# Output blocks and layer 1's q, k transposed by DMA, and score matmuls that alternate between the array's halves

## The chip, the cores and the metric

The kernel runs on one core of a Trainium2 chip. The engines named below are TensorE (PE; PEld is its weight load), VectorE (DVE), ScalarE (ACT), GpSimd (POOL) and SyncE (SP), which here issues nearly all DMAs. The metric is the device time of one execution in microseconds. The time before is 2124.01 us, the median of 3 runs (2122.88 to 2124.37).

## The reference

A decoder trunk of two layers over 256 positions of 2048 features, batch 1, in float32. Layer 0 mixes by sliding-window attention (16 heads of 64, four to a key head) beside an mLSTM; layer 1 by a causal attention with forget gates (16 heads of 128). Each layer then has a SwiGLU feed-forward part with 5632 hidden features. Cut to what matters here:

```python
def sliding_window_attention(q, k, v, sinks):          # HEAD_DIM = 64, window 128
    scores = jnp.einsum('bnqhgd,bnkhd->bnhgqk', qb, kb) * (HEAD_DIM ** -0.5)
    scores = scores - slopes * dist.astype(jnp.float32)
    ...
def forgetting_attention_mixer(xn, w_in, b_f, w_out):  # FOX_HEAD_DIM = 128
    proj = xn @ w_in
    q, k, v, f = split_cols(proj, FOX_SIZES)
    ...
        s = jnp.einsum('bhqd,bhkd->bhqk', qb, k) * scale
        s = s + cb[..., None] - c[:, :, None, :]
    ...
    return out @ w_out
def swiglu(xn, w_gate, w_up, w_down):
    return (jax.nn.silu(xn @ w_gate) * (xn @ w_up)) @ w_down

for layer in range(2):
    xn = rms_norm(h, norm_mix[layer])
    mix = swa_mlstm_mixer(xn, ...) if layer == 0 else forgetting_attention_mixer(xn, ...)
    h = h + mix
    h = h + swiglu(rms_norm(h, norm_ffn[layer]), w_gate[layer], w_up[layer], w_down[layer])
return rms_norm(h, norm_final)
```

## The kernel before

**Precision and tiles.** Every large product is made of float32 values split into a high and a low part (type fp32r): three matmuls, high by high, high by low and low by high, in place of one. The residual `h` lies in SBUF as 2 row tiles of 128 positions by 2048 features. Matmuls contract over features on the partitions, so their left operand has to lie with features on the partitions: `xh`, `xl` hold the scaled input in that form, 16 tiles of 128 features by 256 positions, and `mh`, `ml` the mixer's or the hidden layer's output.

**Weights.** `load_raw` (L103) issues a DMA from SP of a chunk, 256 rows by 512 columns; `split_chunk` (L158) makes `hi` on ACT (L161) and `lo` on DVE (L162). There are 4 raw buffers and 6 of each split form. `gemm` (L177) walks the chunks, 12 matmuls each (L192 to L194); `project` runs 8 chunks into 2 accumulators of 128 by 512.

**How work is ordered.** The engines have queues of their own. The order of instructions on each is fixed when the kernel is built, by a planner that plays the program through with its own model of times; an instruction of a later piece of code may so stand before one of an earlier piece. In addition, the code keeps lists of work that falls due later: an entry is a step number and a function, and `run_due` (L172) calls it when the loop reaches that step, placed after the latest cast of a weight chunk.

**From rows to columns.** There are two ways. One is on TensorE: eight matmuls against an identity make four tiles of a block of 512 features in PSUM (L245 in `split_scaled`, L306 in `transpose_many`), which ACT and DVE then scale, split or copy out. The other is by DMA: the float32 block is taken apart on ACT into two planes of 16-bit halves (L272, or L521 in the feed-forward part), four transposing DMAs on SP turn them (L274, L523), and later a `join` on ACT puts the halves together again (L279, L528) and hands the block on. `split_turned` (L268) is this second way for a block of `h`; `scrap` (L284) gives it its two buffers, borrowed from the pool of the feed-forward part.

**Output projection.** `out_proj` (L386) runs two passes over pairs of blocks of 512 features, (0, 1) and (2, 3). In a pass both blocks do 6 chunks each, then the last 2 chunks each. After a block, `add_out` adds it into `h`. Blocks 0 and 1 go by `split_turned`, with their joins due at steps 6 and 10 of the second pass (`LATER`); blocks 2 and 3 go by `split_scaled` on TensorE.

**Feed-forward part.** `ffn` (L473) has three parts of 3, 4 and 4 groups of 512 hidden features, each followed by two groups of the down projection. A group (`pair_group`, L409) takes 8 pairs of feature tiles in the order `ORDER`. A plain pair is 24 matmuls. A mixed pair, marked 1 in `ORDER`, works with sums and differences of tiles and of weights (7 products instead of 8, so 21 matmuls): it needs sums of the pair's columns (`sums_of`, into `sx`) and four more subtractions and two more splits of the weights on DVE and ACT. Its products use the four PSUM banks that the plain accumulators of the group before had. After the last pair, the products are added into `c` (L466 to L470), the plain accumulators too (L494), and `silu` and the product are formed. A group's result is turned by DMA, with the join in the next group.

**Layer 1's attention.** For each of 4 groups of 4 heads (L910 to L938): project q, transpose it on TensorE into `qt`, project k, transpose it into `kt`, project v, then `attention` (L309).

**Scores.** `attention` works on 4 heads. It takes heads 0 and 2 first, then 1 and 3: for each such half, two narrow score matmuls (L316, 128 keys), one DVE instruction, two wide ones (L323, 256 keys), one DVE instruction. Each float32 matmul shows as two instructions. In layer 0 a head has 64 rows, and head j lies in rows 0 to 63 for even j and 64 to 127 for odd j of the partitions (`half_of`).

## Time and profile before

| What | us |
|---|---|
| Median of 3 runs | 2124.01 |
| Profiled execution, its own time | 2122.88 |
| Its span, first instruction to last | 2121.2 |
| PE, busy | 2105.2 |
| DVE, busy | 1719.5 |
| ACT, busy | 1277.0 |
| One transpose of a q or k block of layer 1 (L306, 64 in all), listed mean | 0.272 |
| One transpose of a block of `h` (L245, 88 in all), listed mean | 0.300 |
| Plane copy and joining copy of a block of the hidden layer, each of two | 1.04 and 1.35 |
| Transposing DMA, issue to landing, median (100 in all) | 2.5 |
| Weight chunk of 512 KB, issue to landing, median | 3.6 to 4.8 |

The span is the time from the first instruction to the last in one profiled execution; the execution took 1.7 us more. Busy times of engines overlap, so they don't add up. A listed length of an instruction is from its start to its end; on TensorE the next one starts before the last has ended, so the same line can be listed long and cost little. In a row of the list of groups, "x64" is the number of instructions. The granted TensorE clock is 0.999 of full speed throughout.

### The profile page before, as it was taken

The page shows a single profiled execution, that of the slowest core. Times are in us where ns is not written, and L with a number is a line of the kernel's source. Part 1 is how long each engine was busy: PE and PEld are TensorE (multiplying, and loading weights), DVE is VectorE, ACT ScalarE, POOL GpSimd, SP SyncE. Part 2 cuts the span into 40 slices and gives each one's busy share as a digit, 9 for nine tenths or more (in the row PEclk, how much of TensorE's full clock was granted, in tenths as well). Part 3 has the DMA queues.
Part 4 walks back from the last instruction along what each step waited for, and adds up shares of the span by engine and source line. Part 5 has one row for each costly group of instructions (what it writes and reads, how often), then busy time and mean ns, then how long its engine had stood idle before and what let it go on. Part 6 is the DMA issues. An engine that isn't in the chain of part 4 may idle for free.

```text
span 2121.2 us, 26858 instructions
## 1 busy us (share of the span) xinstructions
PE 2105.2 (99%) x9699; PEld 1747.9 (82%) x9699; DVE 1719.5 (81%) x2212; ACT 1277.0 (60%) x1612; POOL 39.6 (2%) x61
## 2 busy tenths in 40 slices
PE   8999999999999999999999999999999999999998
PEld 7888888888888888888888888888888888888886
DVE  6665558999999999999855554579999999989994
ACT  6565457765567656766645544576755667556763
POOL 2110000000000000000000000000000000000000
PEclk9999999999999999999999999999999999999999
DMA  8454547666567666666575564676656666656754
GB/s 267 145 157 149 170 149 268 209 203 215 191 211 225 215 207 216 209 202 215 163 231 168 169 179 140 194 237 210 215 196 208 218 196 224 225 188 212 224 182 147
DMA packets 267942, 421.48 MB, mean 199 GB/s; under 512 B 67136, under 2 KB 75424, under 8 KB 267552
## 3 DMA queue, kind: packets, MB, share of 16 engines
q1 hardware_dynamic: 267136, 416.02, 61.6%
q0 software_dynamic: 624, 3.72, 0.5%
q8 instruction: 76, 1.25, 0.2%
q14 instruction: 58, 0.48, 0.1%
q10 hardware_dynamic: 48, 0.02, 0.0%
HBM read 404.48 MB, written 2.11 MB: 192 GB/s over the span
## 4 chain that ended last, share of the span: by engine, by line
PE 98%; ACT 1%; issue 0%; DMA 0%; DVE 0%; DVEq 0%; POOLq 0%; POOL 0%; ACTq 0%
PE acc L402 17%; PE acc L403 17%; PE acc L404 17%; PE acc L192 10%; PE acc L193 10%; PE acc L194 10%; PE prod L402 4%; PE prod L403 4%; PE prod L404 4%; PE p L323 1%; PE ptm L306 1%; PE po L374 1%; PE pt L245 0%; PE pp L366 0%; PE p L316 0%
## 5 line engine op out<-in xcount | busy, mean ns | idle before, releaser
L161 ACT CAST hi<-raw 128x1024 fp32r<-128x1024 f32 (+2 forms) x681 | 692.5, 1032 | 598.5 <-PE acc L404 307.6
L162 DVE TENSOR_TENSOR lo<-raw,hi 128x1024 fp32r<-128x1024 f32 (+2 forms) x681 | 807.3, 1201 | 259.5 <-ACT hi L161 256.2
L403 PE MATMUL acc<-lo,xh 128*128 128x512 f32 x946 | 368.1, 389 | 0.0
L402 PE MATMUL acc<-hi,xh 128*128 128x512 f32 x946 | 367.4, 389 | 0.0
L404 PE MATMUL acc<-hi,xl 128*128 128x512 f32 x946 | 366.8, 389 | 0.0
L192 PE MATMUL acc<-hi,xh 128*128 128x512 f32 (+3 forms) x736 | 275.8, 377 | 0.8 <-ACT hi L161 0.8
L193 PE MATMUL acc<-lo,xh 128*128 128x512 f32 (+3 forms) x736 | 275.8, 375 | 0.0
L194 PE MATMUL acc<-hi,xl 128*128 128x512 f32 (+3 forms) x736 | 275.5, 376 | 0.0
L404 PEld LDWEIGHTS acc<-hi,xl 128*128 128x128 f32 x946 | 177.6, 188 | 36.9
L402 PEld LDWEIGHTS acc<-hi,xh 128*128 128x128 f32 x946 | 177.5, 188 | 36.8
L403 PEld LDWEIGHTS acc<-lo,xh 128*128 128x128 f32 x946 | 177.6, 188 | 36.7
L403 PE MATMUL acc<-lo,mh 128*128 128x512 f32 x437 | 170.0, 389 | 0.0
L402 PE MATMUL acc<-hi,mh 128*128 128x512 f32 x437 | 168.1, 389 | 0.0
L404 PE MATMUL acc<-hi,ml 128*128 128x512 f32 x437 | 167.9, 389 | 0.0
L192 PEld LDWEIGHTS acc<-hi,xh 128*128 128x128 f32 x736 | 138.7, 189 | 24.8 <-ACT hi L161 1.2
L193 PEld LDWEIGHTS acc<-lo,xh 128*128 128x128 f32 x736 | 139.0, 189 | 24.2 <-issue 0.9
L194 PEld LDWEIGHTS acc<-hi,xl 128*128 128x128 f32 x736 | 138.8, 189 | 24.5 <-issue 0.8
L295 DVE TENSOR_TENSOR lt<-raw,ht 128x1024 fp32r<-128x1024 f32 x95 | 115.9, 1220 | 15.6 <-ACT ht L294 15.6
L294 ACT CAST ht<-raw 128x1024 fp32r<-128x1024 f32 x95 | 99.8, 1050 | 45.7 <-PE acc L404 26.9
L192 PE MATMUL acc<-hi,mh 128*128 128x512 f32 x320 | 125.3, 392 | 1.2 <-ACT mh L294 1.2
L193 PE MATMUL acc<-lo,mh 128*128 128x512 f32 x320 | 125.3, 392 | 0.0
L194 PE MATMUL acc<-hi,ml 128*128 128x512 f32 x320 | 123.9, 390 | 0.0
(313 smaller groups left out, 3120.4 us busy)
## 6 DMA issues: line engine op xcount, KB each, us to landing
raw<-in_w_gate_dram SPq DMA_DIRECT2D x176, 512.0 KB, 4.4
raw<-in_w_up_dram SPq DMA_DIRECT2D x176, 512.0 KB, 4.7
raw<-in_w_down_dram SPq DMA_DIRECT2D x176, 512.0 KB, 4.8
raw<-in_w_in_odd_dram SPq DMA_DIRECT2D x88, 512.0 KB, 3.9
raw<-in_w_in_even_dram SPq DMA_DIRECT2D x64, 512.0 KB, 4.1
raw<-in_w_out_even_dram SPq DMA_DIRECT2D x32, 512.0 KB, 3.6
raw<-in_w_out_odd_dram SPq DMA_DIRECT2D x32, 512.0 KB, 4.1
raw<-in_w_in_odd_dram SPq DMA_DIRECT2D x8, 272.0 KB, 2.8
```

The source lines that it names most:

```text
L161: latest[0] = nc.scalar.copy(hi[:, :, 0:n], raw[:, :, 0:n])
L162: nc.vector.tensor_tensor(out=lo[:, :, 0:n], in0=raw[:, :, 0:n], in1=hi[:, :, 0:n].bitcast(F32), op=ALU.subtract)
L192: nc.tensor.matmul(o, ah[:, ts], hi, start=(k == 0), stop=False)
L193: nc.tensor.matmul(o, ah[:, ts], lo, start=False, stop=False)
L194: nc.tensor.matmul(o, al[:, ts], hi, start=False, stop=(k == k_all - 1))
L294: nc.scalar.copy(dst_h, src)
L295: nc.vector.tensor_tensor(out=dst_l, in0=src, in1=dst_h.bitcast(F32), op=ALU.subtract)
L306: nc.tensor.transpose(pt[:, i, :], s_, ident)
L323: nc.tensor.matmul(p1[:, jj, :], q_of(j, 1), k_of(j), start=True, stop=True)
L402: nc.tensor.matmul(o, ah, hi, start=start, stop=False)
L403: nc.tensor.matmul(o, ah, lo, start=False, stop=False)
L404: nc.tensor.matmul(o, al, hi, start=False, stop=stop)
```

## The change

Four things are changed.

1. In layer 1, q and k of the first three groups of heads are turned by DMA, by a new function `turn`, with the join due at step 6 of the projection that follows. The fourth group stays on TensorE.
2. In `out_proj`, blocks 2 and 3 go by `split_turned` too. Their joins are handed to the feed-forward part and fall due at positions 3 and 5 of its first group. `scrap` gives block 2 the buffer of block 0 and block 3 the two buffers of `sd`, which are allocated later and share their tag.
3. `ORDER` has its mixed pairs at positions 1, 3, 5 (pairs 1, 3, 5) in place of 2, 4, 6 (pairs 2, 3, 6).
4. `attention` first issues the narrow score matmuls of heads 0, 1, 2, 3, in two PSUM tiles by parity, and the two DVE instructions for them, then the wide ones likewise.

```diff
-ORDER = ((0, 0), (0, 1), (1, 2), (0, 4), (1, 3), (0, 5), (1, 6), (0, 7))
+ORDER = ((0, 0), (1, 1), (0, 2), (1, 3), (0, 4), (1, 5), (0, 6), (0, 7))
...
-LATER = (6, 10)
+AHEAD = 6
+LATER = (6, 10, 3, 5)
...
     def scrap(fp, n):
-        if n == 0:
+        if n % 2 == 0:
             box = fp.tile([P, 4, NB], F32, tag="c", name="box", bufs=1)
             halves = box[:, 0:2, :], box[:, 2:4, :]
+        elif n == 3:
+            halves = [fp.tile([P, 3, NB], F32, tag=f"sd{i}", name="box", bufs=1)[:, 0:CK, :] for i in range(2)]
         else:
...
         s = sp.tile([P, 4, 3 * P], F32, tag="s", name="s", bufs=2)
-        for half in range(2):
-            hs = slice(half, 4, 2)
-            p0 = pm.tile([P, 2, P], F32, tag="pm", name="p0")
-            for jj in range(2):
-                j = 2 * jj + half
-                nc.tensor.matmul(p0[:, jj, :], q_of(j, 0), k_of(j)[:, 0:P], start=True, stop=True)
-            nc.vector.scalar_tensor_tensor(
-                out=s[:, hs, 0:P], in0=p0, scalar=scale, in1=bias0[:, hs, :], op0=ALU.mult, op1=ALU.add
-            )
...
+        for b, cols, bias in ((0, P, bias0), (1, S, bias1)):
+            pq = [pm.tile([P, 2, cols], F32, tag="pm", name=f"p{b}") for _ in range(2)]
+            for j in range(4):
+                nc.tensor.matmul(pq[j % 2][:, j // 2, :], q_of(j, b), k_of(j)[:, 0:cols], start=True, stop=True)
+            for half in range(2):
+                hs = slice(half, 4, 2)
+                nc.vector.scalar_tensor_tensor(
+                    out=s[:, hs, b * P : b * P + cols],
+                    in0=pq[half],
...
     def out_proj(w, idx, key, extra):
-        last = KT - 4
+        last, rest = KT - 4, []
...
-                if n0 == 0:
-                    later.append((LATER[i], split_turned(idx, i, *scrap(extra[2], i), extra)))
-                else:
-                    split_scaled(idx, n0 + i, extra)
+                (later if n0 == 0 else rest).append(
+                    (LATER[n0 + i], split_turned(idx, n0 + i, *scrap(extra[2], n0 + i), extra))
+                )
                 square_sum(key, n0 + i)
+        return rest
...
-    def ffn(layer, fp, sx, sd, key, idx_next=None, key_next=None, finish=None):
+    def ffn(layer, fp, sx, sd, key, todo, idx_next=None, key_next=None, finish=None):
...
-            todo = []
             for g in range(g0, g1):
...
-            sd = [fp.tile([P, nd, 4, P], F32R, name=f"sd{i}", bufs=1) for i in range(2)]
-            out_proj(w_out, idx, key, (*sx, fp))
-            ffn(layer, fp, sx, sd, key, **rest)
+            todo = out_proj(w_out, idx, key, (*sx, fp))
+            sd = [fp.tile([P, nd, 4, P], F32R, tag=f"sd{i}", name=f"sd{i}", bufs=1) for i in range(2)]
+            ffn(layer, fp, sx, sd, key, todo, **rest)
...
+        def turn(src, dst):
+            planes = od.tile([P, 2, NT, NB], U16, tag="planes", name="planes")
+            turned = od.tile([P, 2, 4, NT, P], U16, tag="turned", name="turned")
+            su = src.bitcast(U16).rearrange("p t (n b) -> p t n b", b=2)
+            for b in range(2):
+                nc.scalar.copy(planes[:, b, :, :], su[:, :, :, b])
+                for t in range(NT):
+                    nc.sync.dma_start_transpose(turned[:, b, :, t, :], planes[:, b, t, :])
+
+            def join():
+                du = dst.rearrange("p k s -> p (k s)").bitcast(U16).rearrange("p (n b) -> p n b", b=2)
+                for b in range(2):
+                    nc.scalar.copy(du[:, :, b], turned[:, b, :, :, :].rearrange("p k t q -> p (k t q)"))
+
+            return join
+
         for i in range(4):
...
                 n_ = nat1(project(wi1, off + i * NB, NB), NB, "qk")
+                if i < 3:
+                    later.append((AHEAD, turn(n_, dst)))
+                    continue
```

More of the change, by code (lines that the diff above doesn't have):

```diff
@@ L310, in attention @@
         s = sp.tile([P, 4, 3 * P], F32, tag="s", name="s", bufs=2)
-        for half in range(2):
-            hs = slice(half, 4, 2)
-            p0 = pm.tile([P, 2, P], F32, tag="pm", name="p0")
-            for jj in range(2):
-                j = 2 * jj + half
-                nc.tensor.matmul(p0[:, jj, :], q_of(j, 0), k_of(j)[:, 0:P], start=True, stop=True)
-            nc.vector.scalar_tensor_tensor(
-                out=s[:, hs, 0:P], in0=p0, scalar=scale, in1=bias0[:, hs, :], op0=ALU.mult, op1=ALU.add
-            )
-            p1 = pm.tile([P, 2, S], F32, tag="pm", name="p1")
-            for jj in range(2):
-                j = 2 * jj + half
-                nc.tensor.matmul(p1[:, jj, :], q_of(j, 1), k_of(j), start=True, stop=True)
-            nc.vector.scalar_tensor_tensor(
-                out=s[:, hs, P : 3 * P], in0=p1, scalar=scale, in1=bias1[:, hs, :], op0=ALU.mult, op1=ALU.add
-            )
+        for b, cols, bias in ((0, P, bias0), (1, S, bias1)):
[7 more added lines that the diff above has]
+                    in0=pq[half],
+                    scalar=scale,
+                    in1=bias[:, hs, :],
+                    op0=ALU.mult,
+                    op1=ALU.add,
+                )
         parts = (slice(0, P), slice(P, 3 * P))
@@ L394, in out_proj @@
                 add_out(accs[i], n0 + i)
-                if n0 == 0:
-                    later.append((LATER[i], split_turned(idx, i, *scrap(extra[2], i), extra)))
-                else:
-                    split_scaled(idx, n0 + i, extra)
+                (later if n0 == 0 else rest).append(
+                    (LATER[n0 + i], split_turned(idx, n0 + i, *scrap(extra[2], n0 + i), extra))
+                )
                 square_sum(key, n0 + i)
+        return rest
     def three(o, ah, al, hi, lo, start, stop):
```

## The prediction

> **What bounds the kernel now.** I read the page's busy times and its chain first: which engine the end waits for.

> ```profile
> PE 2105.2 (99%) x9699; PEld 1747.9 (82%) x9699; DVE 1719.5 (81%) x2212; ACT 1277.0 (60%) x1612; POOL 39.6 (2%) x61
> PE 98%; ACT 1%; issue 0%; DMA 0%; DVE 0%; DVEq 0%; POOLq 0%; POOL 0%; ACTq 0%
> ```

> TensorE is busy for 2105.2 of 2121.2 us and is 98% of the chain, so a microsecond of its work that goes is a microsecond of time, as long as the others keep supplying it. A listed matmul time is not its cost, though: instructions overlap. The cost is the distance between starts, read in the timeline of PE around the transposes of one query block (start, length, instruction):

> ```profile
> 1076.02 0.39 PE L193 MATMUL acc<-lo,xh 128*128 128x512 f32 x1
> 1076.25 0.38 PE L306 MATMUL ptm<-ident,qk 128*128 128x128 f32 x2
> 1076.38 0.48 PE L194 MATMUL acc<-hi,xl 128*128 128x512 f32 x1
> 1076.70 0.39 PE L192 MATMUL acc<-hi,xh 128*128 128x512 f32 x1
> ...
> 1077.16 0.39 PE L194 MATMUL acc<-hi,xl 128*128 128x512 f32 x1
> 1077.39 0.82 PE L306 MATMUL ptm<-ident,qk 128*128 128x128 f32 x6
> 1077.96 0.48 PE L192 MATMUL acc<-hi,xh 128*128 128x512 f32 x1
> 1078.28 0.39 PE L193 MATMUL acc<-lo,xh 128*128 128x512 f32 x1
> ```

> Undisturbed, matmuls start 0.227 us apart. With two transposes between, L194 comes 0.36 after L193 and its successor 0.32 later: 0.13 + 0.09 lost. With six, L192 comes 0.80 after L194 and its successor 0.32 later: 0.57 + 0.09. Eight transposes cost 0.88 us; no wait for data is in it.

> Then the same for one sliding-window attention, whose heads have 64 rows:

> ```profile
> 69.23 0.39 PE L194 MATMUL acc<-hi,xl 128*128 128x512 f32 x1
> 69.55 0.71 PE L316 MATMUL p<-ks,qt 64*128 64x128 f32 x4
> 70.10 0.38 PE L323 MATMUL p<-ks,qt 64*128 64x256 f32 x1
> 70.10 0.37 PE L316 MATMUL p<-ks,qt 64*128 64x128 f32 x1
> ...
> 70.65 1.03 PE L323 MATMUL p<-ks,qt 64*128 64x256 f32 x5
> 71.61 0.50 PE L192 MATMUL acc<-hi,xh 128*128 128x512 f32 x1
> ```

> At 70.10 an L323 of heads 0, 2 and an L316 of heads 1, 3 start together: the two halves of the array work at once, but the second half starts only 0.55 us after the first.

> Last, what feeds PE: the waits (us in total, times, longest), the timelines of SP and ACT round one existing turn by DMA, and the stage table for one feed-forward group at the start and one in the middle.

> ```profile
> ACT hi L161 <- PE acc L404: 307.6, 211, 3.5
> SPq L523 <- ACT c L521: 62.0, 20, 4.2
> ```

> ```profile
> 437.07 5.45 SPq L523 DMA_TRANSPOSE turned<-c  x4
> 436.00 2.00 ACT L521 COPY c<-c 128x1024 uint16<-128x1024 uint16 x2 [0.48 <-DVE c L498]
> 451.02 2.56 ACT L528 COPY c<-turned 128x1024 uint16<-128x1024 uint16 x2
> ```

> ```profile
> 353.00:394.00 41.00, 41.00 (x185) 34.00 (x183) 39.15 (x56) 27.25 (x35) 0.69 (x1) 1.00 0.63 200
> 634.00:675.50 41.50, 41.50 (x185) 34.38 (x184) 39.82 (x51) 28.52 (x32) 0.00 (x0) 1.00 0.69 215
> ```

> Casts wait for PE to release one of six chunk buffers: ACT runs up to six chunks ahead, 6 x 12 matmuls x 0.227 = 16 us. Columns three to six of the table are PE, PEld, DVE, ACT: in the groups DVE is 96% busy (39.82 of 41.5), nearly a second bound, ACT only 69%.

> **Transposes.** They go for q and k of three groups of layer 1 (6 blocks) and for output blocks 2, 3 of both layers (4 blocks): 80 instructions. Six blocks at 0.88 are 5.3; the four output blocks, read in the same way, are 0.90, 0.90, 0.98 and 0.89, 3.7 together: **-9.0 us**. [...]

> What replaces them, per block: two plane copies on ACT (2.00), four transposing DMAs on SP (5.45), the last landing about 2.5 after its issue, two joining copies (2.56). ACT gains 4.56 x 10 = 46 us, DVE loses twelve L307 copies of 0.69 (8 us), the SP queue gets 40 issues (54 us). DVE's scaled splits at the layer ends stay (0.48 from either source). None is on the path while the lead holds:

> *SP.* Behind a transpose that waits for its planes stand weight loads. Held 4.2 (the longest wait so far) + 5.45 = 9.7 us, they use up the four raw buffers ahead (4 x 2.72 = 10.9, less 4 of landing) and then 2.8 of the 16 us of split chunks. Twenty existing turns do so with no gap on PE.

> *Layer 1.* A k block has nat1 2 x 0.69 + 2.00 + landing 6.7 (437.07 to 443.75) + 2.56 = 12.6 us before its attention, and the v projection takes 96 x 0.227 = 21.8: 9 us of slack; q has 31. ACT is 8.64 of 22 us busy here. The join stands in ACT's order behind the cast of chunk 6; if the DMA has not landed, later casts queue behind it for at most 6.7 us, within 16.

> *Layer ends.* Block 2 is ready 5.4 us before the last output matmul, block 3 with it. Two adds 1.36, planes 2.00, landing 6.7, join 2.56, scaling 4 x 0.5 make 14.6 us: ready at +9 and +15, SP's second four adding 5. First use is pair 4 (+20.4 us, 90 matmuls) and pair 6 (+30.6). ACT's load in that group rises from 27.25 by about 9 (one block's planes 2.0, two joins 5.1, half of the scaling) to 36 of 41 us. Waits for two landings (13.4) would make 50, 9 over; the lead covers that barely. Bounds per layer: 0 and 9 us; I take 0.3, since the existing joins of blocks 0, 1 load ACT likewise (41.95 of 57 us in 296 to 353) and PE shows no gap. **+0.6 in both.**

> **Score matmuls.** The four attentions cost, against undisturbed matmuls, 2.26, 2.75, 2.26, 2.99: 10.3 us (69.23 to 71.61 is 2.38, less 0.227, plus 0.11 on the next). The longer ones are split, their last four L323 issued later. One half's own work is 4 x 0.111 + 4 x 0.216 = 1.31. Alternating lets both halves start together: 0.55 less each, 1.71, or about 2.1 if bank waits still split the narrow from the wide. Saved: 3.4 or 2.7; **-3.0**. Ends: 4.2 (1.31 + 0.2 of entry and exit each) and 0. A low and a high instruction of one head share a half; if nothing starts past a waiting one, eight take five slots instead of four, 0.33 worse, and about 1.7 is saved; I give this 1 in 10, inside the forecast's own range. [...] The layer 1 heads have 128 rows: same matmuls, same starts, nothing.

> **The order of pairs.** Five plain and three mixed pairs either way: 183 matmuls, 41.5 us. But the first mixed pair of a group moves from position 2 to 1. Its products need the banks that DVE's L494 adds drain: now 8.9 us pass (adds end at 662.84, products start at 671.79), then 3.5, a pair being 5.45. The down groups already have this order: near 706 two adds run at 706.06 while products start at 706.47, and PE shows no gap. Cost 0; without that cover, what DVE is late.

> Sum: 2121.2 - 9.0 - 3.0 + 0.6 = 2109.8 span. The profiled execution took 2122.88, 1.7 more, and the median of the runs is 1.1 above it: **2112.6**.

> **Rivals.** *A, the scores gain nothing* (bank waits or the planner's order keep the halves apart): 2115.6. For: two of four are split already. Against: the halves overlap at 70.10. 7%.
> *B, the layer ends starve*: casts queue behind joins that wait for landings. If the lead covers 6 of the 9 us, 3 per layer are lost in place of 0.3: 2118; if none, 2130. For: ACT at 36 of 41. Against: smaller bursts left no gap. 14%, spread over 2114 to 2124.
> *C, slower*: DVE, 96% busy, drains the banks too late at the 16 boundaries between gate/up groups and 4 from down to gate/up. It decides from 3.5 us of slip; 4.4 us costs 0.9 each, 18 us: 2130. For: DVE's load, and the two blocks' splits now fall into the first group. Against: the down groups. 9%.
> *D, each transpose frees its listed 0.272 us*: 80 x 0.272 = 21.8 instead of 9.0, 2100. The starts exclude it nearly: 2%.

> **Chances.** The forecast has 68% (its own range 2109 to 2115.5). 0.2% (4.2 us) is about what a measurement can tell from no change: faster is below 2119.8, slower above 2128.3. Faster: 68 + 7 + 9 of B + 2 = 86%; same: 5 of B; slower: C, 9%. Range 2108.5 to 2119: the forecast, A and most of B's lower part; the low end is 9.0 + 4.2 with no new wait (2110.8), less 2 for what the planner may close elsewhere.

> **What would show it.** Right: L306 of qk falls from 64 to 16 and L245 from 88 to 56; PE stays above 98% in the chain; the first L316 of both halves start within 0.2 us; four attentions near 1.7 to 2.1; the first group of each layer still 41.5 long. Wrong: idle before PE at the first products of a group (C), before pairs 4 to 6 after the output projection or before layer 1's scores (B), or score lines one half after the other (A).

## The result, and the profile after

The changed kernel takes 2112.44 us, median of 4 runs (2112.13 to 2113.81), beside 2123.74 for the kernel before on the same chip (4 runs): a ratio of 0.9948, interval 0.9932 to 0.9964. Its profiled execution took 2112.37 us with a span of 2110.7, 10.5 less than before.

The page of the changed kernel, busy times and chain, and two rows of its list of groups:

```profile
PE 2094.8 (99%) x9619; PEld 1740.2 (82%) x9619; DVE 1711.7 (81%) x2200; ACT 1312.1 (62%) x1650; POOL 37.8 (2%) x61
PE 99%; DMA 0%; ACT 0%; issue 0%; DVE 0%; DVEq 0%; POOLq 0%; POOL 0%; ACTq 0%
...
L309 PE MATMUL ptm<-ident,qk 128*128 128x128 f32 x16 | 2.4, 272 | 0.0
L246 PE MATMUL pt<-ident,h 128*128 128x128 f32 x56 | 9.9, 315 | 1.3 <-DMA h<-in_x_dram 1.3
```

Eighty matmuls are gone (9619 for 9699; 64 to 16 and 88 to 56), PE's busy time falls by 10.4 us, and PE still makes up the whole chain. ACT has 35 us more work, DVE 8 less.

Stage by stage, between the same PE instructions of the two profiles:

| Stretch | Before | After | Difference |
|---|---|---|---|
| Start to first matmul of layer 0's output projection | 252.80 | 251.68 | -1.12 |
| From there to that of layer 1 | 1078.66 | 1071.16 | -7.49 |
| From there to the last matmul | 780.66 | 778.75 | -1.91 |
| Behind the last matmul | 9.06 | 9.06 | 0 |

From the first output projection on, 9.40 us are saved, and that is the transposes. The stage table of the changed kernel, for the first feed-forward group and one in the middle (columns as before: length, PE, PEld, DVE, ACT, POOL, clock, DMA share, GB/s), and its longest kind of wait on ACT:

```profile
350.00:391.00 41.00, 41.00 (x183) 33.95 (x182) 38.51 (x55) 34.53 (x45) 0.69 (x1) 1.00 0.78 227
634.00:675.50 41.50, 41.50 (x185) 34.37 (x184) 39.11 (x50) 28.40 (x32) 0.00 (x0) 1.00 0.70 213
```

```profile
ACT hi L162 <- PE acc L405: 244.1, 176, 4.2
```

ACT's load in the first group has risen from 27.25 to 34.53 of 41 us, and PE is busy in all of it: no gap. ACT waits less often for PE to release chunk buffers (244.1 us in 176 waits, 307.6 in 211 before): part of its lead over PE is used up.

One sliding-window attention of the changed kernel, on PE's timeline (start, length):

```profile
69.03 0.39 PE L195 MATMUL acc<-hi,xl 128*128 128x512 f32 x1
69.35 1.58 PE L317 MATMUL p<-ks,qt 64*128 64x128 f32 x16
70.86 0.50 PE L193 MATMUL acc<-hi,xh 128*128 128x512 f32 x1
71.20 0.40 PE L194 MATMUL acc<-lo,xh 128*128 128x512 f32 x1
```

All sixteen matmuls of this attention stand in one run, as they did before (69.55 to 71.61), but the first matmuls of the two halves now start 6 ns apart. L193 comes 1.83 us after L195 and its successor 0.34 later: 1.60 + 0.11 = 1.71 above undisturbed matmuls, 0.55 less than before.

The clock is not at full speed throughout any more. Stage tables of the kernel before, then of the changed one, for the same stretches:

```profile
181.00:186.00 5.00, 5.00 (x24) 4.14 (x24) 3.29 (x8) 3.30 (x5) 0.00 (x0) 1.00 0.11 23
186.00:190.00 4.00, 4.00 (x23) 3.06 (x22) 2.49 (x9) 0.34 (x2) 0.00 (x0) 1.00 0.73 240
```

```profile
181.00:186.00 5.00, 5.00 (x26) 4.09 (x25) 3.50 (x13) 1.49 (x5) 0.00 (x0) 0.86 0.53 176
186.00:190.00 4.00, 4.00 (x16) 3.12 (x16) 2.22 (x3) 2.23 (x5) 0.00 (x0) 0.75 0.00 0
```

The mean granted clock (third column from the right) is 0.86 and 0.75 in the changed kernel, though PE is busy throughout; the clock's record shows one stretch of 3.41 us at 0.5, from 184.58 to 188.00. PE's timeline there, in the changed kernel:

```profile
182.35 0.36 PE L727 MATMUL pn<-ident,edge 4*128 4x4 f32 x2
182.58 1.97 PE L750 MATMUL pb<-mt,sel 4*128 4x256 f32 x8
185.19 0.77 PE L193 MATMUL acc<-hi,xh 128*128 128x512 f32 x1
...
186.19 0.63 PE L195 MATMUL acc<-hi,xl 128*128 128x512 f32 x1
186.62 0.63 PE L193 MATMUL acc<-hi,xh 128*128 128x512 f32 x1
```

L193 comes 0.43 us after L195, where 0.227 is usual. Five such steps lose 0.2 each, the transposes at 184.48 and the step behind them the other 0.55: 1.55 us in all. Ahead of it stand 3.3 us of matmuls with four rows or four columns, which come from the mLSTM's decays (L725 to L727 and L750).

### The profile page after: what moved, and what is told of

Its sections match the earlier page's. It is cut to its first block, busy times and chain, and to the rows that moved or that the text cites. A ratio compares the mean times of both kernels' runs of the same rounds, so it can differ in the third digit from the quotient of the medians.

```text
span 2110.7 us, 26839 instructions
## 1 busy us (share of the span) xinstructions
PE 2094.8 (99%) x9619; PEld 1740.2 (82%) x9619; DVE 1711.7 (81%) x2200; ACT 1312.1 (62%) x1650; POOL 37.8 (2%) x61
## 4 chain that ended last, share of the span: by engine, by line
PE 99%; DMA 0%; ACT 0%; issue 0%; DVE 0%; DVEq 0%; POOLq 0%; POOL 0%; ACTq 0%
PE acc L405 17%; PE acc L403 17%; PE acc L404 17%; PE acc L193 11%; PE acc L195 11%; PE acc L194 11%; PE prod L405 4%; PE prod L403 4%; PE prod L404 4%; PE p L317 1%; PE po L375 1%; PE ptm L309 0%; PE pp L367 0%; PE pt L246 0%; PE po L376 0%; DMA h<-in_x_dram 0%
## 5 line engine op out<-in xcount | busy, mean ns | idle before, releaser
L162 ACT CAST hi<-raw 128x1024 fp32r<-128x1024 f32 (+2 forms) x681 | 694.9, 1032 | 546.5 <-PE acc L405 244.1
L404 PE MATMUL acc<-lo,xh 128*128 128x512 f32 x946 | 368.0, 389 | 0.0
L193 PE MATMUL acc<-hi,xh 128*128 128x512 f32 (+3 forms) x736 | 275.7, 377 | 0.8 <-ACT hi L162 0.8
L194 PE MATMUL acc<-lo,xh 128*128 128x512 f32 (+3 forms) x736 | 275.8, 375 | 0.0
L195 PE MATMUL acc<-hi,xl 128*128 128x512 f32 (+3 forms) x736 | 275.5, 376 | 0.0
L404 PEld LDWEIGHTS acc<-lo,xh 128*128 128x128 f32 x946 | 177.6, 188 | 36.9
L404 PE MATMUL acc<-lo,mh 128*128 128x512 f32 x437 | 169.7, 389 | 0.0
L193 PEld LDWEIGHTS acc<-hi,xh 128*128 128x128 f32 x736 | 138.9, 189 | 25.7 <-ACT hi L162 1.2
L195 PEld LDWEIGHTS acc<-hi,xl 128*128 128x128 f32 x736 | 139.0, 189 | 25.0 <-issue 1.2
L194 PEld LDWEIGHTS acc<-lo,xh 128*128 128x128 f32 x736 | 139.3, 189 | 23.9 <-issue 0.2
L193 PE MATMUL acc<-hi,mh 128*128 128x512 f32 x320 | 125.2, 391 | 1.2 <-ACT mh L297 1.2
L194 PE MATMUL acc<-lo,mh 128*128 128x512 f32 x320 | 125.3, 392 | 0.0
L195 PE MATMUL acc<-hi,ml 128*128 128x512 f32 x320 | 123.8, 389 | 0.0
L298 DVE TENSOR_TENSOR lt<-t,ht 128x1024 fp32r<-128x1024 f32 x95 | 115.9, 1220 | 5.5 <-ACT ht L297 5.5
L297 ACT CAST hi<-raw 128x512 fp32r<-128x512 f32 x95 | 59.0, 621 | 97.6 <-PE acc L405 87.8
```

Source lines behind the costliest of these rows:

```text
L162: latest[0] = nc.scalar.copy(hi[:, :, 0:n], raw[:, :, 0:n])
L193: nc.tensor.matmul(o, ah[:, ts], hi, start=(k == 0), stop=False)
L194: nc.tensor.matmul(o, ah[:, ts], lo, start=False, stop=False)
L195: nc.tensor.matmul(o, al[:, ts], hi, start=False, stop=(k == k_all - 1))
L297: nc.scalar.copy(dst_h, src)
L298: nc.vector.tensor_tensor(out=dst_l, in0=src, in1=dst_h.bitcast(F32), op=ALU.subtract)
```

## The experiments

The theory was the prediction's: each part has its own price on PE, and the new work elsewhere is covered, at the layer ends barely. The rivals to tell apart were that part of the saving is not the transposes', that DVE is nearly late at group boundaries (C), and that the layer ends starve (B).

**One part at a time.** *Scores only* (the kernel before, with the new loop of `attention`):

```diff
-        for half in range(2):
-            p0 = pm.tile([P, 2, P], F32, tag="pm", name="p0")
...
+        for b, cols, bias in ((0, P, bias0), (1, S, bias1)):
+            pq = [pm.tile([P, 2, cols], F32, tag="pm", name=f"p{b}") for _ in range(2)]
+            for j in range(4):
+                nc.tensor.matmul(pq[j % 2][:, j // 2, :], q_of(j, b), k_of(j)[:, 0:cols], start=True, stop=True)
```

> The kernel before with the new order of score matmuls alone. Theory (what counts is the distance between starts on PE, and the supply is covered): in the trace of the changed kernel two of the four sliding-window attentions take 1.71 us in place of 2.26, and the two that are split take as long as before (2.53 and 2.97), so 1.1 us go: span 2120.1. Rival (the split is made by other parts of the change, and the prediction's 3.0 us hold for this part alone): 2118.2, with no attention split. Layer 1's score matmuls stay at 2.6 us each in both.

Measured: 2122.11 us, ratio 0.9992 (0.9983 to 1.0002), span 2120.2. The start stretch is 0.94 shorter, with one clock window at half in it; the rest is as before. The ratio's interval includes no change, so the gain of the scores is read from the trace alone. The ten runs are not alike: two of them, the only ones with a mean granted clock of 0.999, take 2118.75 and 2118.98, the other eight 2121.41 or more.

*Layer 1's q, k only* (`turn` and its use for the first three groups):

```diff
+                if i < 3:
+                    later.append((AHEAD, turn(n_, dst)))
+                    continue
```

> The kernel before with q and k of three groups of layer 1 turned by DMA, and nothing else. Theory: 48 transposes go, six blocks at 0.88 us, 5.3 us: span 2115.9, no idle time on PE before layer 1's scores. Rival (the 27 us of copies on ACT and 33 us of issues on SP are not covered): PE gaps at the projections and a span over 2117. Second rival (the 8 us of copies that DVE no longer does shorten layer 1 as well): under 2115.

Measured: 2117.85 us, ratio 0.9975 (0.9966 to 0.9984), span 2116.0. From the first output projection on 5.65 us are saved: six blocks at 0.94.

*The order of pairs only*:

```diff
-ORDER = ((0, 0), (0, 1), (1, 2), (0, 4), (1, 3), (0, 5), (1, 6), (0, 7))
+ORDER = ((0, 0), (1, 1), (0, 2), (1, 3), (0, 4), (1, 5), (0, 6), (0, 7))
```

> The kernel before with the new order of pairs alone (mixed at positions 1, 3, 5); blocks 2 and 3 still go through TensorE. Theory: 183 matmuls a group either way and the banks are drained in time, span 2121.2 within 0.4. Rival C of the prediction (DVE drains the banks late where a mixed pair comes second): idle time on PE at the first products of groups, up to 0.9 us at each of 20 boundaries, span up to 2139.

Measured: 2124.59 us, ratio 1.0007 (0.9997 to 1.0016); the span of 2123.1 misses the 2121.2 expected. From the first output projection to the last matmul the two kernels differ by 0.06 us. The rest lies outside: +0.74 at the start, where a clock window costs 1.6 and the first attention comes 0.87 earlier, and +1.18 behind the last matmul, of which the cause stays open. The order costs nothing on PE between these marks, and C falls.

*Output blocks 2, 3 and the order* (the diff of `out_proj`, `scrap` and `ffn`, and `ORDER`):

```diff
-                if n0 == 0:
-                    later.append((LATER[i], split_turned(idx, i, *scrap(extra[2], i), extra)))
-                else:
-                    split_scaled(idx, n0 + i, extra)
+                (later if n0 == 0 else rest).append(
+                    (LATER[n0 + i], split_turned(idx, n0 + i, *scrap(extra[2], n0 + i), extra))
+                )
```

> The changed kernel without the new scores and without turns of q and k: output blocks 2 and 3 by DMA, and the new order of pairs. Theory: 32 transposes go, 0.90 + 0.90 + 0.98 + 0.89 = 3.7 us: span 2117.5, first group of each layer without a gap although the lead falls to 4.5 us. Rival B of the prediction (casts behind joins that wait for landings starve the first group): 0.3 to 3 us lost per layer, 2118 to 2123.5.

Measured: 2119.33 us, ratio 0.9982 (0.9973 to 0.9991), span 2118.1. Layer 0's blocks give 1.83 us and layer 1's 1.91; the start, without a slow clock window, is 0.6 longer. So 5.65 + 1.83 + 1.91 = 9.39 is the whole of the 9.40 in the changed kernel: nothing was lost or gained between the parts.

**How far the cover reaches: fewer chunk buffers.** Both kernels with four buffers of each split form instead of six:

```diff
-    wp = ctx.enter_context(tc.tile_pool(name="wp", bufs=6))
+    wp = ctx.enter_context(tc.tile_pool(name="wp", bufs=4))
```

Changed kernel:

> The changed kernel with 4 in place of 6 buffers of split weight chunks, so that ACT and DVE run two chunks (5.4 us) less ahead of PE. Theory (the added copies on ACT and issues on SP cost nothing only because of the lead): the smallest lead in the first feed-forward group, 4.5 us with six buffers, goes below nothing; idle time on PE of 1 to 4 us per layer at the layer end and some at the turns of layer 1, so that the span is 2 to 10 us more than the 2110.7 with six, and the gap to the kernel before with 4 buffers falls under 9 us. Rival (ACT has 30% idle time anyway, the lead does not matter): the gap to the kernel before with 4 buffers stays 10 to 11 us.

Kernel before:

> The kernel before with 4 in place of 6 buffers of split weight chunks. Theory: it loses less than the changed kernel does, 0 to 5 us over 2121.2, since its first feed-forward groups keep a lead of 8 us and more with six buffers. Rival: it loses as much as the changed kernel.

Measured: the changed kernel 2118.61 us (0.9977, 0.9967 to 0.9987), span 2117.6, 6.9 longer than with six; the kernel before 2133.64 (two runs; 1.0048, 1.003 to 1.0067), span 2131.0, 9.8 longer. It went the other way round: the kernel before needs the buffers more. PE's waits, first in the kernel before with four buffers and then PE's timeline at one of its places:

```profile
PE acc L192 <- ACT hi L161: 2.1, 4, 0.8
PE acc L193 <- DVE lo L162: 1.5, 4, 0.5
PE prod L403 <- DVE lt L295: 0.8, 3, 0.3
```

```profile
982.63 0.50 PE L402 MATMUL acc<-hi,mh 128*128 128x512 f32 x1
983.40 0.50 PE L403 MATMUL prod<-lt,sd 128*128 128x512 f32 x1 [0.27 <-DVE lt L295]
```

The first two lines have their like in the changed kernel (2.3 and 1.5 us); the third falls at the first mixed pair of a down group. At 982.63 the next matmul comes 0.77 us later, in place of 0.23, and waits for a weight difference of a mixed pair. The old order has its last mixed pair at position 6, which leaves two plain pairs (position 7 and the down group's position 0) ahead of the down group's first mixed pair; the new order has it at 5, which leaves three. PE loses 2.8 us at four of the six such places in the kernel before, and none there in the changed kernel. That the order makes it is argued from the place: the new order alone was not run with four buffers. So this test says that the new order is likely the gentler one for DVE. It says little on the layer ends: both kernels lose 1.6 us at the output projection of layer 0 (at 320), and the changed one loses only 0.6 at the first products of a layer's first group.

**How far the cover reaches: the new work twice.** In the changed kernel, the ten new turns issue their plane copies and their four DMAs a second time, with the same data:

```diff
-            for b in range(2):
-                nc.scalar.copy(planes[:, b, :, :], su[:, :, :, b])
-                for t in range(NT):
-                    nc.sync.dma_start_transpose(turned[:, b, :, t, :], planes[:, b, t, :])
+            for _ in range(2):
+                for b in range(2):
+                    nc.scalar.copy(planes[:, b, :, :], su[:, :, :, b])
+                    for t in range(NT):
+                        nc.sync.dma_start_transpose(turned[:, b, :, t, :], planes[:, b, t, :])
```

> The changed kernel, with the plane copies and the four transposing DMAs of output blocks 2, 3 (both layers) and of q, k of three groups of layer 1 issued twice: 20 more plane copies of about 1 us on ACT (20 us) and 40 more DMAs on SP (54 us); the joins stay single. Theory (these ten turns are wholly covered, with lead to spare): from the end of the first output projection on the same length as the changed kernel within 0.5 us, span 2109.5 to 2111.5 depending on the clock window at the start. Rival (the lead covers them barely, as the prediction has it): a doubled turn delays its join by 2 us of planes and 5.5 of issues, PE runs dry at the layer ends and the length from there on grows by 3 us or more, with PE waits of over 0.5 us on DVE or ACT in the first feed-forward groups.

Measured (one execution): 2125.88 us, span 2124.1, 13.4 longer than the changed kernel. Layer 0's feed-forward part is 8.45 us longer, layer 1's end 3.91; from layer 1's forget gates (L889, at 1059.26) to its output projection, where all turns of q and k lie, the length is 263.58 us in both, to 0.01. So the turns of q and k are covered with room for twice the work, and those at the layer ends are not: the rival of this run. ACT's timeline of this kernel in the first group, and what PE then does:

```profile
372.02 1.04 ACT L298 CAST ht<-raw 128x1024 fp32r<-128x1024 f32 x1
375.93 2.52 ACT L281 COPY box<-box 128x1024 uint16<-128x1024 uint16 x2 [2.87 <-DMA box<-box]
378.32 0.60 ACT L298 CAST sx<-s 128x512 fp32r<-128x512 f32 x1
```

```profile
374.27 0.39 PE L404 MATMUL acc<-ht,xh 128*128 128x512 f32 x1
378.97 0.79 PE L404 MATMUL acc<-hi,sx 128*128 128x512 f32 x1 [4.32 <-ACT sx L298]
379.57 0.63 PE L405 MATMUL acc<-lo,sx 128*128 128x512 f32 x1
```

ACT stands before the join of block 3 (L281) until its DMA lands, 2.87 us; behind the join in ACT's order stands the cast of a mixed pair's column sums (L298), and PE waits 4.32 us for that cast. From 377.6 on, within that wait, the clock is at half for 6.83 us (mean granted clock 0.51 from 377.6 to 384.5), which the 0.79 and 0.63 lengths show. In the changed kernel itself the same cast stands here (ACT's timeline, then PE's):

```profile
363.24 2.58 ACT L280 COPY box<-box 128x1024 uint16<-128x1024 uint16 x2
...
369.71 0.60 ACT L297 CAST sx<-s 128x512 fp32r<-128x512 f32 x1
```

```profile
372.98 0.39 PE L403 MATMUL acc<-hi,sx 128*128 128x512 f32 x1
```

Ready at 370.31, used at 372.98: 2.7 us of lead is what the changed kernel has left there.

Then the DMAs alone twice, for blocks 2 and 3 of both layers, with the plane copies once:

```diff
-            for t in range(NT):
-                nc.sync.dma_start_transpose(turned[:, b, :, t, :], planes[:, b, t, :])
+            for _ in range(2 if n >= 2 else 1):
+                for t in range(NT):
+                    nc.sync.dma_start_transpose(turned[:, b, :, t, :], planes[:, b, t, :])
```

> The changed kernel, with the four transposing DMAs of output blocks 2 and 3 of both layers issued twice, the plane copies once: 16 more issues on SP, 5.1 to 5.9 us per block, nothing more on ACT. In the changed kernel the last of these DMAs is issued at 357.1 and lands near 359.6, the join of block 3 starts on ACT at 363.2, and the first product that needs the sums cast behind it starts 3.2 us after they are ready. Theory (what is late is the landing, and the casts that stand behind the join on ACT): the landing moves by 10 to 11 us, 3.7 of which are slack before the join and 3.2 behind it, so PE waits 2 to 5 us once in the first feed-forward group of layer 0 and up to as much in layer 1, each followed by two clock windows at half (3.1 us): 5 to 14 us longer from the first output projection's end on. Rival (the plane copies on ACT and their waits for the first turn were late in the kernel with both doubled): no PE wait above 0.6 us in the first groups, the length as in the changed kernel within 1 us.

Measured (one execution): 2119.85 us, span 2118.1. From the first output projection on it is 6.8 longer (4.77 in layer 0, 2.00 in layer 1), within the theory's 5 to 14; but not by one wait of 2 to 5 us. The queue of SP, and three waits of PE over this kernel:

```profile
345.43 22.12 SPq L276 DMA_TRANSPOSE box<-box  x16
```

```profile
PE acc L405 <- DVE lo L299: 0.9, 1, 0.9
PE acc L404 <- ACT hi L162: 0.9, 2, 0.5
PE prod L405 <- DVE lt L299: 0.5, 2, 0.3
```

The planner put all sixteen DMAs in one run of 22 us without a weight load between. The sums' cast (371.30) is not late: it ends at 371.91 and its product starts at 373.48. Weights are, as DVE's timeline shows behind that run:

```profile
371.65 0.69 DVE L442 TENSOR_TENSOR t<-raw 128x512 f32<-128x512 f32 x1 [3.69 <-DMA raw<-in_w_up_dram]
```

PE then has several short waits, with one clock window at half in layer 0 (mean granted clock 0.57 from 377 to 381). So the DMAs alone cost 6.8 of the 12.4 that the full doubling cost. That the other 5.6 come with the second plane copies is not shown, since the planner orders the two kernels differently: in one a landing holds a cast, in the other the queue of SP holds weight loads. Either way a turn at a layer end can be late.

**The scores' order.** The changed kernel with heads 0, 2, 1, 3 in place of 0, 1, 2, 3, so that four instructions of one half of the array stand ahead of the other half's:

```diff
-            for j in range(4):
+            for j in (0, 2, 1, 3):
```

> The changed kernel with the score matmuls of a width in the order of heads 0, 2, 1, 3 in place of 0, 1, 2, 3. Theory (matmuls of the other half of the array start ahead of up to three that wait, as the trace of before shows): the second half starts about 0.1 us after the first in place of 0.01, and a whole attention takes 1.7 to 1.9 us as against 1.71. Rival (a half starts only when all instructions before it have started, so alternation itself is what helps): the second half starts 0.45 us later, 2.1 us and more.

Measured (one execution): 2113.41 us. PE's timeline of the first attention:

```profile
68.24 0.39 PE L195 MATMUL acc<-hi,xl 128*128 128x512 f32 x1
68.56 1.68 PE L317 MATMUL p<-ks,qt 64*128 64x128 f32 x16
70.17 0.50 PE L193 MATMUL acc<-hi,xh 128*128 128x512 f32 x1
```

L193 comes 1.93 after L195, 1.70 + 0.11 = 1.81 above undisturbed, only 0.1 more than alternating. The second half does not wait until the first half's four are done: its first matmul starts 13 ns after the first half's (6 ns when alternating). Nor is it enough that the sixteen stand together, since they do so in the kernel before too and cost 2.26. What counts is how many instructions of one half the code puts ahead of the other half's first: eight cost 2.26 (the kernel before), four 1.81, two 1.71. The rows do not name the half, and the planner orders PE; that it kept the code's order of the scores is read from these differences.

**Towards a faster kernel.** The split attentions lack a bank. A first attempt takes the fourth score tile from the accumulators' pool, and turns three more blocks by DMA (q, k of the fourth group; block 1 of layer 0's down projection):

```diff
-            pq = [pm.tile([P, 2, cols], F32, tag="pm", name=f"p{b}") for _ in range(2)]
+            pq = [pm.tile([P, 2, cols], F32, tag="pm", name=f"p{b}") for _ in range(2 - b)]
+            if b:
+                pq.append(pa.tile([P, 2, cols], F32, tag="acc", name="p1"))
...
-                    if n < 1:
-                        todo.append((LATER_DOWN[n], split_turned(idx_next, n, *scrap(fp, n))))
+                    if n < 2:
+                        todo.append((LATER_DOWN[n], split_turned(idx_next, n, *scrap(fp, 5 * n))))
...
-                if i < 3:
+                if i < 4:
```

> The changed kernel with three additions: one of the four score tiles of an attention comes from the other PSUM pool, so that it need not wait for the output of the attention before; q and k of the fourth group of layer 1 are turned by DMA too; block 1 after the last down projection of layer 0 is turned by DMA, in buffers of the sums that are no longer read. Theory: the two split attentions fall from 2.53 and 2.97 to about 1.7 (-2.1), two blocks go (-1.6, one of them costs 0.7 where the matmuls are narrower), one more (-0.8): span 2106.2. Rival (k of the fourth group is not ready in time, since its v projection is only half as wide: 12.6 us against 11.4; or the accumulators' pool is needed by the projection): a wait on PE of 1 to 5 us, 2107 to 2111.

Measured: 2135.14 us, ratio 1.0049 (1.0035 to 1.0062), a miss. PE's longest waits:

```profile
PE pp L369 <- DVE s L361: 16.1, 2, 8.5
```

The score tile holds a bank of the next projection's accumulators, so PE has nothing to do until the softmax on DVE is through: it is idle for 8.5 and 7.6 us. The mean granted clock of its profile is 0.991, of the changed kernel's 0.998. The extra bank itself does what it should: all four attentions have their sixteen score matmuls in one run here (at 59.56, 76.78, 106.84 and 124.57), none is split. The start is 25.9 us longer than in the changed kernel. But from the first output projection on this kernel is 2.8 faster, so the three further blocks alone are worth having:

> The changed kernel, with two more blocks kinds turned by DMA: q and k of the fourth group of layer 1's heads (2 blocks), and block 1 of the down projection of layer 0 (1 block). Three blocks at 0.88 to 0.94 us of transposes: theory -2.8 us against the changed kernel, span about 2107.9 with a clock window at 0.5 at the start, 2106.4 without; all of it between the end of the first output projection and that of the second (1071.2 becomes 1068.4). Rival: the last group's turn comes too late for the output projection's first products or the extra join of the down block delays layer 1's first projection: a PE gap of 1 us or more there, no gain.

Measured: 2110.49 us (2110.22 to 2111.41), ratio 0.994 (0.9926 to 0.9953). From the first output projection to the last matmul it is 2.43 shorter than the changed kernel, 2.8 expected, and PE has no wait there that the changed kernel lacks. The start has two clock windows at half instead of one (mean granted clock 0.77 from 181 to 186 and 0.50 from 186 to 190); so the span is 2109.7 where 2107.9 was expected.

Last, the same kernel with the four-row matmuls of the decay kept apart from the four-column ones:

```diff
-            for g in range(2):
+            def decay(g):
...
             transpose_many(qst, [qsc[:, hh, :] for hh in range(ML_H)])
+            decay(0)
             km = natural(mp, project(wi, OFF_KM, NB), NB, "km")
...
+            decay(1)
             for c in range(NT):
                 pq = pm.tile([P, ML_H, P], F32, tag="pm", name="pq")
```

> The kernel with the three more blocks by DMA, and in layer 0's mLSTM the four-row matmuls of the decay (pb, two tiles of four instructions) moved from right behind the four-column ones (pn): the first behind the transposes of q, the second behind those of k, so that no clock window of 3.41 us holds more than about 1.3 us of such small matmuls in a row. Theory (small matmuls for over about 2 us of one window halve the next window's clock): no stretch below full clock after the start; the section up to the output projection is 250.1 plus or minus 0.7 in place of the changed kernel's 251.7, span about 2106.4. Rival (the dip has another cause, or any small matmuls at all bring it): the clock falls to half for a window near 185 us as before, span 2107.9 or more.

Measured: 2109.41 us (2108.47 to 2109.92), ratio 0.9934 (0.9921 to 0.9946), span 2106.9. Stage table of this kernel:

```profile
181.00:186.00 5.00, 5.00 (x27) 4.30 (x28) 3.73 (x12) 1.27 (x2) 0.00 (x0) 1.00 0.38 121
186.00:190.00 4.00, 4.00 (x19) 2.98 (x19) 2.12 (x4) 1.06 (x1) 0.00 (x0) 1.00 0.47 137
```

The clock stays at 1.00, and the start takes 249.91 us, as the theory has it (250.1 plus or minus 0.7). The profiles differ by 2.8 us, two windows of about 1.5; the medians differ by 1.08 and the intervals overlap. The mean granted clock of each run, of which one slow window takes 0.0008, fits: 0.999 in all five runs here, 0.997 or 0.998 in all five without the move and in all four of the changed kernel. All five of its times lie below all four of the changed kernel: this is the fastest version here.

## Why the prediction held, and where it did not

| Term (us) | Predicted | Measured |
|---|---|---|
| Transposes | -9.0 | -9.40 (q, k 5.65; output blocks 1.83 and 1.91) |
| Score matmuls | -3.0 | -1.1 in the four attentions |
| New waits at the layer ends | +0.6 | 0 |
| Order of pairs | 0 | 0 (0.06 alone) |
| Clock window at half | none | +1.55 |
| Rest of the start | none | -1.57 |
| Span | -11.4 | -10.5 |

**Transposes.** The reading by starts holds: 0.94 per block against 0.88 to 0.98. The listed length (rival D, 22 us) is far off.

**Score matmuls.** The mechanism was right and the size was not. Where all sixteen stand together they save the 0.55 that the prediction gave for each, and they come to its 1.71. What failed is the assumption that this holds for all four, or at worst 2.1. Two attentions stay split, at 2.53 and 2.97 us; read by the same rule, the two split ones of the kernel before are 2.53 and 2.99, so the 2.75 of the prediction for the first was 0.22 too much. The changed kernel's PE and then its DVE, round one of them:

```profile
150.13 1.57 PE L317 MATMUL p<-ks,qt 64*128 64x128 f32 x12
153.21 1.13 PE L317 MATMUL p<-ks,qt 64*128 64x256 f32 x4
```

```profile
151.26 0.68 DVE L298 TENSOR_TENSOR ml<-po,mh 128x512 fp32r<-128x512 f32 x1
151.86 0.74 DVE L320 SCALAR_TENSOR_TENSOR s<-p,bias 128x256 f32<-128x256 f32 x2
```

Twelve matmuls go at 150.13, and the last four three microseconds later. The pool has four banks. One still holds the output `po` of the attention before, which DVE reads until 151.94 (L298); the fourth score tile has to wait for it, and the planner has filled the time with others. The kernel that takes its fourth tile from another pool bears this out: there no attention is split. The prediction had priced the bank waits as the narrow tiles delaying the wide ones, within one attention; it is the previous attention that holds the bank. Its variant of 1.7 saved, if nothing passes a waiting matmul, is not what happened: that would cost 0.33 in each, and the unsplit ones have none of it.

**New waits.** Price and mechanism of rival B are now measured. "The lead covers that barely" was right: 2.7 us of lead are left before one product of the first group, and doubling the turns makes PE wait 4.3 there. The 0.3 a layer was the wrong end of a range from 0 to 9; at exactly this load it is 0. The cover of layer 1's q and k (9 us of slack in the prediction) holds even with its work doubled.

**Order.** Rival C falls twice: the new order alone costs 0.06 us, and with fewer buffers it is the old one that makes PE wait for DVE. The prediction looked only at the start of a group, where the first mixed pair comes one pair earlier, and not at its end, where the last one does too and leaves one more plain pair ahead of the down groups.

**The start.** The table's two lines above the span were not foreseen, and nearly cancel. The first is the clock. The second is read by the distances between starts as well. About 0.6 us is a by-product of the planner: before, the products of one attention (L374, L375) alternate with four-column matmuls of the gates and the stretch takes 3.45 us, now it takes 2.83. Another 0.7 lies at the softmax transposes of the second attention, first in the kernel before, then in the changed one:

```profile
113.00 0.30 PE L366 MATMUL pp<-ident,s 128*128 128x128 f32 x1 [0.18 <-DVE s L358]
```

```profile
110.05 0.27 PE L367 MATMUL pp<-ident,s 128*128 128x128 f32 x1
```

Before, PE waits there for DVE, and from the matmul ahead of these twelve transposes (112.43) to the second one behind them (115.38) 2.95 us pass; now there is no wait, and it is 2.25. The kernel with the new scores alone has both savings (-0.94 = -1.1 + 1.55 - 1.4), and q, k only, the order only and the blocks with the order have neither: both come with the new scores. The last 0.2 lies ahead of the first attention, which follows the moment at which the clock first reaches full speed by about half: it starts at 69.55 with full speed from 14.26 us (the kernel before), at 69.35 from 13.91 (the changed one), at 68.44 from 12.00 (q, k only) and at 70.09 from 14.95 (the blocks with the order). This differs between profiles whatever the change.

**The time.** The span came out 0.9 above the 2109.8 predicted, and the median 0.2 below the 2112.6: the prediction added 1.1 because the median of the kernel before was that much above its profiled execution, and in the changed kernel the two agree (2112.44 and 2112.37). Part of the close agreement is this cancelling, and the span's is luck too: the scores saved 1.9 less than predicted and the clock took 1.55, against 0.4 more from the transposes, 0.6 without the new waits and 1.57 at the start.

## What to carry to other kernels

## What was not expected of the hardware

**A clock that slows under a busy PE.** Wherever a profile here has slow stretches near the mLSTM's decays, they last 3.41 us or 6.83, twice that, and they begin a whole number of 3.4133 us after the clock first went to full speed, to within 0.01 (in the changed kernel at 184.58, fifty of them behind 13.91). How much of the 3.3 us of tiny matmuls (four rows or four columns) falls into one such window decides. Of the 14 profiles, eleven hold 2.04 us or more of them in one window at full clock and have a slow window right behind it (3.28 in the changed kernel, 2.76 in q, k only, 2.04 in the order 0, 2, 1, 3). Three hold at most 1.72 in any window and have none (the kernel before 1.65, the blocks with the order 1.72, the kernel with the decay's matmuls kept apart 1.45). The mean granted clocks of these profiles are 0.991 to 0.998 in the eleven and 0.999 in the three. Whether it is the few rows or the few columns was not tried apart. The windows' phase follows the start-up, so a kernel can have the slow window in one execution and not in another, as the ten runs of the scores alone suggest (mean granted clock 0.999 in two of them, 0.997 or 0.998 in eight). A slow stretch was seen at a real pause too: in the doubled kernel PE waits 4.32 us, up to 378.97, and the clock was at half from 377.6 on, for 6.83 us.

**Two halves that pass each other.** Matmuls of 64 rows in different halves start 6 ns apart when alternated, and when four of one half stand ahead of the other's the attention costs only 0.10 us more (1.81 for 1.71). Each head's matmul is two instructions in one half, so a start 6 ns behind the first one is another head's, ahead of the first head's second instruction, which starts 0.21 us after the first (69.35 and 69.56 in the changed kernel). In the kernel before, the L316 at 70.10 starts ahead of three L323 that the code issues earlier. By the rival of the grouped order's run the second half would have waited for the first half's four, and 2.1 or more would have come out; it is 1.81. The run of the grouped order is one execution.
